# An expert stage whose engines keep a written order, with eight pairs of split weights instead of five

## The chip, the cores and the metric

The kernel runs on one core of one Trainium2 chip. The metric is the device time of one execution in microseconds (us). Inputs and outputs are float32.

## The reference

One encoder layer: a token mixer (attention beside a gated linear recurrence, merged by gates), then a feed-forward part of 16 experts, in which each expert picks its 128 tokens. The change is in the second part alone:

```python
def expert_choice_ffn(h, w_router, w_gate, w_up, w_down):      # S = 1024 tokens, D = 1024, FF = 2048
    cap = EC_CAPACITY_FACTOR * S // N_EXPERTS                   # 128
    affinity = jax.nn.softmax(logits, axis=-1)
    top_w, top_idx = lax.top_k(affinity.transpose(0, 2, 1), cap)
    xe = jax.vmap(lambda hb, ib: hb[ib])(h, top_idx)            # 16 x 128 x 1024
    hid = jax.nn.silu(jnp.einsum('becd,edf->becf', xe, w_gate)) * jnp.einsum('becd,edf->becf', xe, w_up)
    ye = jnp.einsum('becf,efd->becd', hid, w_down) * top_w[..., None]
    # ye is added to the tokens it came from
```

## The kernel before

**Units.** The expert weights come in 768 units of 128 x 1024 float32 (512 KB): for each of 16 experts 16 units of the gate matrix, 16 of up, 16 of down. An expert is worked in two halves of its FF dimension, so a half has 8 units of each kind. For each unit `eunit` (L1153) loads a raw tile (SyncE's queue, L56), and `split` (L89, L90) makes two tiles of it: `eh`, a cast by ScalarE, and `el` = raw - `eh`, by VectorE. TensorE then does 6 matmuls of 128 x 512: high x high, high x low and low x high, for two column halves. For gate and up they are in `wide` (L1255 to L1257, into PSUM tiles `pg`), for down in `down` (L1218 to L1220, into `py`).

**Buffers.** Raw units go round a ring of 26 tiles (7 of tag `er`, 16 of tag `H`, 3 of tag `er3`); 4 more units are loaded ahead into tiles that later serve for something else (`ye`, `xh`, `xl`, `xg`). Of `eh` and `el` there are 5 pairs (`EB`).

**Other steps of an expert.** `pick` (L1195) makes a one-hot matrix `oh` on VectorE, multiplies it on TensorE (L1202) to get the token indices `idx`, and starts an indirect DMA on GpSimd's queue that gathers the 128 tokens into `xg`. `trans(xg, 8, "x")` turns them on TensorE (8 transposes, L1184, into `tp`) and makes `xh` on ScalarE (L1188) and `xl` on VectorE (L1189), in 8 pieces each; here this is called the x turn. After the gate units of a half, ScalarE makes silu (L1273, `hd`); after its up units VectorE multiplies (L1284). `trans(hd, 4, "h")`, twice in a half, turns the result (8 transposes) and makes `hh` (ScalarE, L89) and `hl` (VectorE, L90); this is the h turn. After the second half's down units VectorE scales `py` into `ye` (L1225), and GpSimd's queue adds it to the output by an indirect DMA (L1226).

**Order.** The program is written gate, down of the half before, up (L1266 on); the h turn is called between gate units 4 and 5, the x turn after the up units of an expert's second half. But in this stage a scheduler orders each engine's instructions by its own estimates, so that what stands in a row on an engine can differ from what is written. Each engine then works through its row in that order, and an instruction that waits holds up all that stand behind it.

Of the kernel before, what the change touches and what calls it, by code (L numbers as in the profile page):

```python
# [9 lines left out]
F32 = mybir.dt.float32  # L10
# [27 lines left out]
def trunk(ctx, tc, t, out, dbg=None):  # L38
# [966 lines left out]
    ER, E3, EB, YB = 7, 3, 5, 1  # L1005

    X2 = dict(er3=E3, ye=YB, xh=2, xl=2)
# [137 lines left out]
    NR = ER + 16 + E3  # L1145
# [3 lines left out]
    def eunit(src):  # L1149
        shape = [P] + list(src.shape)[1:]  # L1150
        j = cnt[0] if cnt[0] < NR else cnt[0] - len(ahead)
        c = j % NR
        if NR <= cnt[0] < NR + len(ahead):  # L1153
            raw = ahead[cnt[0] - NR]
        elif c < ER:
            raw = exr.tile(shape, F32, name="er", bufs=ER)
        elif c >= ER + 16:
            raw = exr.tile(shape, F32, name="er3", tag="er3", bufs=E3)
        else:
            raw = h4("er2", shape, F32)  # L1160
        if not NR <= cnt[0] < NR + len(ahead):
            load(raw, src)
        cnt[0] += 1
        hi = ex1.tile(shape, F32R, name="eh", bufs=EB)
        lo = ex1.tile(shape, F32R, name="el", bufs=EB)
        with ExitStack() as es:
            if cnt[0] <= EB:
                es.enter_context(tc.issue_after(first5[-2]))
                es.enter_context(tc.issue_after(first5[-1]))
            if 3 < cnt[0] <= 24:  # L1170
                es.enter_context(tc.issue_after(held[0]))
            if EB < cnt[0] <= 24:
                es.enter_context(tc.issue_after(held[8]))
            split(raw, hi, lo, nc.gpsimd if cnt[0] <= 3 else None)
        return hi, lo

    def trans(src, n, tag):
        pool = exr if tag == "x" else ex
        hi = pool.tile([P, n, P], F32R, name=tag + "h", tag=tag + "h", bufs=2)
        lo = pool.tile([P, n, P], F32R, name=tag + "l", tag=tag + "l", bufs=2)  # L1180
        for g in range(0, n, 4):
# [3 lines left out]
            if tag == "x":  # L1185
                for c in range(4):
                    k = g + c
                    held.append(nc.scalar.activation(hi[:, k], p[:, c], AF.Identity, bias=mcT[:, k:k + 1], scale=1.0).ins)  # L1188
                    nc.vector.scalar_tensor_tensor(lo[:, k], p[:, c], mcT[:, k:k + 1], hi[:, k].bitcast(F32),  # L1189
                                                   op0=ALU.add, op1=ALU.subtract)  # L1190
            else:
                split(p, hi[:, g:g + 4], lo[:, g:g + 4])
        return hi, lo

    def pick(e):  # L1195

        oh = ex.tile([P, NT, P], BF16, name="oh", bufs=1)
        nc.vector.tensor_tensor(oh, slots[:, None, :].to_broadcast([P, NT, P]),
                                slot[:, :, e:e + 1].to_broadcast([P, NT, P]), ALU.is_equal)
        pi = psE.tile([P, 512], F32, name="tp", bufs=2)  # L1200
# [4 lines left out]
        xg = ex.tile([P, D], F32, name="xg", tag="xg", bufs=2)  # L1205
# [3 lines left out]

    def down(e, fp, hTs, py, ks):  # L1210

        for kk in ks:
            hh, hl = hTs[kk // 4]
            r = kk % 4
            wh, wl = eunit(dunit(e, (fp * 8 + kk) * P))
# [5 lines left out]
        if fp == 1 and ks[-1] == 7:  # L1221
            ye = exr.tile([P, D], F32, name="ye", tag="ye", bufs=YB)
            for n in range(2):
                sl = slice(n * 512, (n + 1) * 512)
                nc.vector.scalar_tensor_tensor(ye[:, sl], py[:, n], tw[:, e:e + 1], g2b[:, sl], op0=ALU.mult, op1=ALU.mult)  # L1225
            nc.gpsimd.indirect_dma_start(out=out, out_offset=bass.IndirectOffsetOnAxis(ap=idx[:, e:e + 1], axis=0),  # L1226
                                         in_=ye, in_offset=None, compute_op=ALU.add)
# [8 lines left out]
    for tag, n, src in (("ye", YB, dunit(0, 2 * P)), ("xh", 2, dunit(0, 3 * P)), ("xl", 2, dunit(0, 4 * P)),  # L1236
                        ("xg", 2, dunit(0, 5 * P))):
# [4 lines left out]
    with tc.high_priority(300):  # L1242
        xparts = trans(pick(0), KT, "x")

    def wide(e, w, fp, parts, between=None):

        xh, xl = parts
        ps = [psE.tile([P, 512], F32, name="pg", bufs=4) for _ in range(2)]
        for k in range(KT):
            if between and k == 4:  # L1250
                between()
            wh, wl = eunit(gunit(e, w, fp, k))
            for n in range(2):
                sl = slice(n * 512, (n + 1) * 512)
                nc.tensor.matmul(ps[n], xh[:, k], wh[:, 0, sl], start=k == 0, stop=False)  # L1255
                nc.tensor.matmul(ps[n], xh[:, k], wl[:, 0, sl], start=False, stop=False)  # L1256
                nc.tensor.matmul(ps[n], xl[:, k], wh[:, 0, sl], start=False, stop=k == KT - 1)  # L1257
        return ps

    def turned(hds):  # L1260
        return [trans(hd, 4, "h") for hd in hds]

    pend = None
    py = None
    for e in range(NE):
        mine = xparts  # L1266
        for fp in range(2):
            turn = []
            gs = wide(e, wg_, fp, mine, (lambda: turn.extend(turned(pend[2]))) if pend else None)
            acts = []  # L1270
            for n in range(2):
                hd = ex.tile([P, 512], F32, name="hd", tag="hd", bufs=3)
                nc.scalar.activation(hd, gs[n], AF.Silu)  # L1273
                acts.append(hd)
            last = e == NE - 1 and fp == 1
            if fp == 0 and e + 1 < NE:
                xg = pick(e + 1)
            if pend and not last:
                if pend[1] == 0:
                    py = psE.tile([P, 2, 512], F32, name="py", bufs=1)  # L1280
                down(pend[0], pend[1], turn, py, range(8))
            us = wide(e, wu_, fp, mine)
            for n in range(2):
                nc.vector.tensor_tensor(acts[n], acts[n], us[n], ALU.mult)  # L1284
            if fp == 1 and e + 1 < NE:
                xparts = trans(xg, KT, "x")
            if last:
                py = psE.tile([P, 2, 512], F32, name="py", bufs=1)
                down(pend[0], pend[1], turn, py, range(4))
                t0 = trans(acts[0], 4, "h")  # L1290
                down(pend[0], pend[1], turn, py, range(4, 8))
# [45 lines left out]
```

## Time and profile before

| | us |
|---|---|
| runs: median (lowest to highest) | 2306.76 (2303.48 to 2307.94) |
| the profiled execution, its device time | 2305.64 |
| its span, first to last instruction | 2303.8 |
| expert stage in it: first gate matmul to last down matmul | 1132.36 to 2291.83 |
| TensorE busy in the span | 2150.1 (93%) |
| VectorE busy | 1868.5 (81%) |
| ScalarE busy | 1383.3 (60%) |

The profile names TensorE's matmuls PE, VectorE DVE, ScalarE ACT, GpSimd POOL and SyncE's queue SPq. A time of an instruction is its start from the begin of the span. Matmuls overlap in the pipeline, so what one costs is read from start to start, not from its duration.

### The profile page before, as it was taken

How to read it: one execution, taken by the hardware profiler on the slowest of the kernel's cores; microseconds unless marked ns; L12 is line 12 of the kernel's file. 1: busy time of each engine (PE TensorE's matmuls, PEld its weight loads, DVE VectorE, ACT ScalarE, POOL GpSimd, SP SyncE). 2: the span in 40 equal slices, each digit the busy share in tenths (PEclk: the TensorE clock that was granted, in tenths of full speed). 3: DMA queues.
4: the chain of work that ended last, by engine and by line, in shares of the span. 5: the costliest groups of instructions: out<-in, count | busy, mean ns of one | idle time of the engine just before them, and what ended most of it. 6: DMA issues, size and time to landing. Idle time of an engine off the chain costs nothing.

```text
span 2303.8 us, 30740 instructions
## 1 busy us (share of the span) xinstructions
PE 2150.1 (93%) x10518; PEld 1718.9 (75%) x10518; DVE 1868.5 (81%) x2601; ACT 1383.3 (60%) x2051; POOL 363.9 (16%) x341
## 2 busy tenths in 40 slices
PE   5998888999999999998499999999999999999997
PEld 4775665788888768897377877778777777777776
DVE  7699998588756465728899999999888898888886
ACT  4657666544433122224477777777777776777675
POOL 5247666000000000005200000000100000000000
PEclk9999999999999999999699999999999999999999
DMA  8111111422231885458589999999999999999992
GB/s 290 58 40 38 38 37 33 142 89 78 97 96 65 257 280 177 136 181 284 181 325 385 365 360 362 369 381 372 338 352 360 367 352 364 354 347 369 355 337 85
DMA packets 208246, 546.84 MB, mean 237 GB/s; under 512 B 19589, under 2 KB 75429, under 8 KB 208090
## 3 DMA queue, kind: packets, MB, share of 16 engines
q1 hardware_dynamic: 185242, 495.08, 59.4%
q0 software_dynamic: 8416, 29.41, 4.5%
q10 hardware_dynamic: 14432, 20.39, 2.5%
q8 instruction: 82, 1.34, 0.2%
q14 instruction: 74, 0.61, 0.1%
HBM read 503.80 MB, written 41.01 MB: 236 GB/s over the span
## 4 chain that ended last, share of the span: by engine, by line
PE 68%; DVE 14%; issue 7%; DMA 5%; ACT 4%; POOL 1%; SPq 0%; ACTq 0%; POOLq 0%; DVEq 0%
PE pg L1256 9%; PE pg L1257 9%; PE pg L1255 9%; PE py L1219 5%; PE py L1220 5%; PE py L1218 4%; DVE Tl L90 3%; PE g L208 2%; PE g L210 2%; PE s L711 2%; PE g L209 2%; DMA wr<-in_ada_w 2%; DVE el L90 2%; DVE mx L567 2%; ACT eh L89 1%
## 5 line engine op out<-in xcount | busy, mean ns | idle before, releaser
L90 DVE TENSOR_TENSOR el<-er,eh 128x1024 fp32r<-128x1024 f32 x761 | 898.1, 1220 | 66.3 <-ACT eh L89 54.6
L89 ACT CAST eh<-er 128x1024 fp32r<-128x1024 f32 x764 | 780.2, 1052 | 144.2 <-PE pg L1257 102.4
L1256 PE MATMUL pg<-el,xh 128*128 128x512 f32 x1024 | 412.0, 403 | 8.6 <-DVE el L90 7.5
L1257 PE MATMUL pg<-eh,xl 128*128 128x512 f32 x1024 | 402.1, 397 | 0.3
L1255 PE MATMUL pg<-eh,xh 128*128 128x512 f32 x1024 | 367.6, 399 | 3.6 <-ACT xh L1188 3.4
L1256 PEld LDWEIGHTS pg<-el,xh 128*128 128x128 f32 x1024 | 192.5, 188 | 65.0 <-DVE el L90 21.7
L1255 PEld LDWEIGHTS pg<-eh,xh 128*128 128x128 f32 x1024 | 192.4, 188 | 53.5 <-ACT xh L1188 7.8
L1257 PEld LDWEIGHTS pg<-eh,xl 128*128 128x128 f32 x1024 | 191.3, 188 | 48.2 <-DVE xl L1189 7.4
L1219 PE MATMUL py<-el,hh 128*128 128x512 f32 x512 | 202.8, 396 | 7.6 <-DVE el L90 7.6
L1218 PE MATMUL py<-eh,hh 128*128 128x512 f32 x512 | 201.5, 394 | 0.8 <-ACT eh L89 0.5
L1220 PE MATMUL py<-eh,hl 128*128 128x512 f32 x512 | 199.8, 390 | 0.0
L208 PE MATMUL g<-hTh,wh 128*128 128x512 f32 x448 | 179.8, 401 | 5.0 <-ACT wh L89 2.9
L210 PE MATMUL g<-hTh,wl 128*128 128x512 f32 x448 | 179.6, 401 | 0.3 <-DVE wl L90 0.2
L209 PE MATMUL g<-hTl,wh 128*128 128x512 f32 x448 | 178.8, 399 | 0.0
L1206 POOL DMA_INDIRECT xg<-d_h,idx x16 | 29.1, 1821 | 804.4 <-DVE idx L1203 678.2
L90 DVE TENSOR_TENSOR Tl<-E,Th 128x512 fp32r<-128x512 f32 x128 | 134.2, 1071 | 2.2 <-ACT Th L89 2.1
L638 POOL TENSOR_TENSOR sum<-sum,E 128x512 f32<-128x512 f32 x84 | 128.2, 1526 | 25.4 <-ACT E L632 20.4
L1219 PEld LDWEIGHTS py<-el,hh 128*128 128x128 f32 x512 | 96.0, 188 | 35.7 <-DVE el L90 15.6
L1218 PEld LDWEIGHTS py<-eh,hh 128*128 128x128 f32 x512 | 96.1, 188 | 25.1 <-ACT eh L89 5.1
L228 ACT ACTIVATE stg<-g 128x512 f32<-128x512 f32 (+1 forms) x78 | 45.1, 578 | 109.3 <-PE g L210 70.1
L1220 PEld LDWEIGHTS py<-eh,hl 128*128 128x128 f32 x512 | 96.2, 188 | 18.8
L90 DVE TENSOR_TENSOR wl<-wr,wh 128x1024 fp32r<-128x1024 f32 x56 | 68.6, 1227 | 43.9 <-ACT wh L89 43.9
(336 smaller groups left out, 3912.3 us busy)
## 6 DMA issues: line engine op xcount, KB each, us to landing
er<-in_w_exp_gate SPq DMA_DIRECT2D x256, 512.0 KB
er<-in_w_exp_up SPq DMA_DIRECT2D x256, 512.0 KB
er<-in_w_exp_down SPq DMA_DIRECT2D x252, 512.0 KB
wr<-in_w_in SPq DMA_DIRECT2D x42, 512.0 KB
wr<-in_ada_w SPq DMA_DIRECT2D x32, 512.0 KB
d_sg<-stg ACTq DMA_DIRECT2D x32, 256.0 KB
sg<-d_sg SPq DMA_DIRECT2D x16, 512.0 KB
d_zq<-stg ACTq DMA_DIRECT2D x24, 256.0 KB
```

The lines of the kernel that those rows point to most:

```text
L89: first = nc.scalar.copy(hi, src)
L90: (eng or nc.vector).tensor_tensor(lo, src, hi.bitcast(F32), ALU.subtract)
L208: nc.tensor.matmul(p, wh[:, k], xT(hTh, n, k), start=k == 0, stop=False)
L209: nc.tensor.matmul(p, wh[:, k], xT(hTl, n, k), start=False, stop=False)
L210: nc.tensor.matmul(p, wl[:, k], xT(hTh, n, k), start=False, stop=k == KT - 1)
L638: (nc.vector if j == NH - 1 else nc.gpsimd).tensor_tensor(a, acc, E, ALU.add)
L1218: nc.tensor.matmul(py[:, n], hh[:, r], wh[:, 0, sl], start=fp == 0 and kk == 0, stop=False)
L1219: nc.tensor.matmul(py[:, n], hh[:, r], wl[:, 0, sl], start=False, stop=False)
L1220: nc.tensor.matmul(py[:, n], hl[:, r], wh[:, 0, sl], start=False, stop=fp == 1 and kk == 7)
L1255: nc.tensor.matmul(ps[n], xh[:, k], wh[:, 0, sl], start=k == 0, stop=False)
L1256: nc.tensor.matmul(ps[n], xh[:, k], wl[:, 0, sl], start=False, stop=False)
L1257: nc.tensor.matmul(ps[n], xl[:, k], wh[:, 0, sl], start=False, stop=k == KT - 1)
```

## The change

It does four things, all in the expert stage.

- **Written order.** The stage becomes a `script`: a list of units and of acts between them. It is emitted inside `in_order(PE, DVE, Activation)`, which ties each instruction of these three engines to the one before it in program order. The split of unit j is emitted in front of unit m as soon as the unit that had its pair before is one of those in front of m (`ensure`).
- **Gate, up, down.** A half is now 8 gate units, silu, 8 up units, the multiply, then the 8 down units of the half before. The h turn stands between up units 4 and 5. The x turn stands between down units 4 and 5 of the half before the one that uses it, and `pick` at the same place one half earlier. `oh` is made after the gate units.
- **Eight pairs.** Five pairs of `eh`, `el` stay as they are; three more take the 7 tiles of tag `er` after the first 7 raw units have left them. The raw ring is then 19 tiles (16 `H`, 3 `er3`); the first 26 loads go where they went. `xg` has one buffer instead of two, so 3 units are loaded ahead instead of 4; `hd` has four instead of three.
- **The x turn's pieces.** All 8 transposes come first, then 8 pieces of `xh`, then 8 of `xl`, instead of `xh` and `xl` by turns.

The number of matmuls, splits, unit loads and indirect DMAs stays the same.

```diff
-    ER, E3, EB, YB = 7, 3, 5, 1
+    EB, MORE, YB = 5, 3, 1
+    RAW = dict(er=7, er3=3)
+    TAGS = ["er"] * 7 + ["H"] * 16 + ["er3"] * 3
+    RING, PAIR = ["H"] * 16 + ["er3"] * 3, "er"
+    PAIRS0 = 7
...
+    def eload(src):
+        shape = [P] + list(src.shape)[1:]
+        j = cnt[0]
+        cnt[0] += 1
+        if NR <= j < NR + len(ahead):
+            return ahead[j - NR]
+        tag = TAGS[j] if j < NR else RING[(j - NR - len(ahead)) % len(RING)]
+        raw = h4("er2", shape, F32) if tag == "H" else exr.tile(shape, F32, name=tag, bufs=RAW[tag])
+        load(raw, src)
+        return raw
+
+    def pair_tag(j):
+        return PAIR if j >= PAIRS0 and (j - PAIRS0) % (EB + MORE) >= EB else None
...
+    def eparts(raw, j):
+        tag = pair_tag(j)
+        if tag:
+            hi, lo = (exr.tile(shape, F32R, name=n, tag=tag, bufs=RAW[tag]) for n in ("eh", "el"))
         else:
+            hi, lo = (ex1.tile(shape, F32R, name=n, bufs=EB) for n in ("eh", "el"))
...
+            split(raw, hi, lo, nc.gpsimd if j < 3 else None)
...
+    for h in range(NH2):
+        e, fp = divmod(h, 2)
+        more = e + 1 < NE
+        for k in range(KT):
+            wide_unit(e, wg_, h, (h, 0), k)
+        act(lambda h=h: silu(h))
+        if more and not fp:
+            act(lambda e=e: set_(ohs, e + 1, lambda: onehot(e + 1)))
+        for k in range(KT):
+            if k == 4:
+                if h:
+                    act(lambda h=h: (turn(h - 1, 0), turn(h - 1, 1)))
+                else:
+                    act(lambda: set_(xgs, 1, lambda: pick(1, ohs[1])))
+            wide_unit(e, wu_, h, (h, 1), k)
+        act(lambda h=h: gated(h))
+        for kk in range(8) if h else ():
+            if kk == 4 and more:
+                if fp:
+                    act(lambda e=e: set_(xparts, e + 1, lambda: trans(xgs[e + 1], KT, "x")))
+                else:
+                    act(lambda e=e: set_(xgs, e + 1, lambda: pick(e + 1, ohs[e + 1])))
+            if kk in (4, 6) and h == NH2 - 1:
+                act(lambda n=kk // 2 - 2: turn(h, n))
+            down_unit(h - 1, kk)
+    for kk in range(8):
+        down_unit(NH2 - 1, kk)
...
+    def ensure(done):
+        while len(parts_) < len(srcs) and before[len(parts_)] < done:
+            parts_.append(eparts(eload(srcs[len(parts_)]), len(parts_)))
...
+    ensure(0)
+    with in_order(ET.PE, ET.DVE, ET.Activation):
+        j = 0
+        for z, run in script:
+            if z is None:
+                run()
+            else:
+                ensure(j)
+                run(*parts_[j])
+                j += 1
```

What this does to the engines' rows is shown at two places. The first is ScalarE's row around the h turn of a late half. A number behind a name tells tiles apart; `er`, `er2` and `er3` are raw tiles. Before:

```order
L89 CAST eh_17673<-er2_17671 128x1024
L89 CAST eh_17685<-er3_17683 128x1024
L89 CAST eh_17697<-er3_17695 128x1024
L89 CAST hh_17719<-tp_17721 128x512
L89 CAST hh_17728<-tp_17730 128x512
L89 CAST eh_17709<-er3_17707 128x1024
L89 CAST eh_17739<-er_17737 128x1024
```

TensorE turns `tp_17721` in the middle of the unit of `eh_17685`, the second gate unit: that unit and one more are split ahead of the turn's cast, and the fourth gate unit's split, `eh_17709`, stands behind it.

After, the same turn of the same engine:

```order
L89 CAST eh_17817<-er2_17815 128x1024
L89 CAST eh_17831<-er2_17829 128x1024
L89 CAST eh_17843<-er2_17841 128x1024
L89 CAST eh_17855<-er2_17853 128x1024
L89 CAST hh_17865<-tp_17867 128x512
L89 CAST hh_17874<-tp_17876 128x512
L89 CAST eh_17885<-er3_17883 128x1024
```

TensorE now turns `tp_17867` behind the fourth up unit, that of `eh_17763`. The seven units that follow on TensorE are split ahead of the turn's cast: four up units (the last is that of `eh_17817`) and three down units (`eh_17831`, `eh_17843`, `eh_17855`).

The second place is TensorE's row around the x turn. Before (expert 6, and so in experts 1 to 6):

```order
L1256 MATMUL pg_14142<-el_14230,xh_13561 128x512
L1257 MATMUL pg_14142<-eh_14229,xl_13562 128x512
L1184 MATMUL tp_14243<-ident_69,xg_13722 128x128 x4
L1184 MATMUL tp_14256<-ident_69,xg_13722 128x128 x4
L1255 MATMUL pg_14269<-eh_14273,xh_14241 128x512
L1256 MATMUL pg_14269<-el_14274,xh_14241 128x512
```

After, an expert's x turn and the matmuls around it:

```order
L1281 MATMUL py_16912<-eh_16858,hl_16839 128x512
L1202 MATMUL tp_16957<-ident_69,xg_16632 128x128 x4
L1202 MATMUL tp_16962<-ident_69,xg_16632 128x128 x4
L1279 MATMUL py_16912<-eh_16870,hh_16847 128x512
L1280 MATMUL py_16912<-el_16871,hh_16847 128x512
...
L1281 MATMUL py_16912<-eh_16908,hl_16848 128x512
L1265 MATMUL pg_17037<-eh_16921,xh_16955 128x512
```

The turn stood right in front of the gate matmul that reads `xh`; now four down units stand between them.

## Rows read from the trace of the kernel before

**Rows 1.** Busy time by stretch of the expert stage (us; in brackets the number of instructions; then the granted TensorE clock as a share of full speed, the mean busy share of the 16 DMA engines, and GB/s). Columns: stretch, its length, PE, PEld, DVE, ACT, POOL.

```profile
1132.36:1200.00 67.64, 67.05 (x301) 53.27 (x300) 60.78 (x69) 54.47 (x67) 1.75 (x1) 0.98 0.82 295
1200.00:1600.00 400.00, 397.06 (x1802) 317.55 (x1801) 373.51 (x386) 316.41 (x358) 24.15 (x12) 1.00 0.99 369
1600.00:2200.00 600.00, 585.52 (x2620) 459.47 (x2619) 530.19 (x568) 442.62 (x530) 34.66 (x16) 1.00 0.97 356
```

**Rows 2.** The same view for one expert each, cut where two successive x turns begin on TensorE: one of the earlier experts, one of the later.

```profile
1404.11:1475.35 71.24, 70.65 (x321) 56.40 (x320) 66.52 (x70) 56.36 (x64) 4.11 (x2) 1.00 0.99 369
1880.98:1954.34 73.36, 71.68 (x322) 56.17 (x320) 64.93 (x70) 53.95 (x65) 4.04 (x2) 1.00 0.99 359
```

**Rows 3.** Waits of SyncE's queue in 1150 to 2304 us (what waited, for whom: us in total, times, longest).

```profile
SPq L56 <- DVE el L90: 704.4, 628, 6.5
```

**Rows 4.** TensorE without a wait: the view by stretch (TensorE alone; us busy, instructions that touch the stretch, clock, DMA share, GB/s) for 72 gate and up matmuls and for 48 down matmuls, each with one that began before; then the instructions in order of time (start, length, what) around an h turn and around a pick.

```profile
1429.95:1446.75 16.80, 16.80 (x73) 1.00 1.03 377
1453.24:1464.14 10.90, 10.90 (x49) 1.00 1.03 410
...
1446.76 1.03 PE L1184 MATMUL tp<-ident,hd 128*128 128x128 f32 x8
1447.55 0.48 PE L1255 MATMUL pg<-eh,xh 128*128 128x512 f32 x1
1447.87 0.40 PE L1256 MATMUL pg<-el,xh 128*128 128x512 f32 x1
...
1418.75 0.35 PE L1202 MATMUL tp<-tq,oh 128*128 128x5 bf16 x8
1418.96 0.47 PE L1218 MATMUL py<-eh,hh 128*128 128x512 f32 x1
1419.28 0.39 PE L1219 MATMUL py<-el,hh 128*128 128x512 f32 x1
```

**Rows 5.** Instructions in order of time as in Rows 4: TensorE from the x turn of an earlier expert to its next h turn; 24 gate matmuls lie between.

```profile
1404.11 1.04 PE L1184 MATMUL tp<-ident,xg 128*128 128x128 f32 x8
1405.68 0.50 PE L1255 MATMUL pg<-eh,xh 128*128 128x512 f32 x1 [0.53 <-ACT xh L1188]
...
1412.27 1.04 PE L1184 MATMUL tp<-ident,hd 128*128 128x128 f32 x8
```

**Rows 6.** Instructions in order of time for a later expert; in brackets the idle time before, and what ended it. First ScalarE and TensorE around an h turn, then VectorE and TensorE around the end of an expert's down units.

```profile
1909.49 1.05 ACT L89 CAST eh<-er 128x1024 fp32r<-128x1024 f32 x1 [0.35 <-PE pg L1257]
1914.60 1.08 ACT L89 CAST hh<-tp 128x512 fp32r<-128x512 f32 x2 [4.05 <-PE tp L1184]
...
1913.96 1.04 PE L1184 MATMUL tp<-ident,hd 128*128 128x128 f32 x8
...
1923.97 0.40 PE L1218 MATMUL py<-eh,hh 128*128 128x512 f32 x1
1924.40 0.50 PE L1256 MATMUL pg<-el,xh 128*128 128x512 f32 x1
1924.74 0.39 PE L1257 MATMUL pg<-eh,xl 128*128 128x512 f32 x1
...
1936.77 1.41 DVE L1225 SCALAR_TENSOR_TENSOR ye<-py,tw,g2b 128x512 f32<-128x512 f32 x2 [1.51 <-PE py L1220]
...
1939.36 0.50 PE L1256 MATMUL pg<-el,xh 128*128 128x512 f32 x1 [0.77 <-DVE el L90]
```

**Rows 7.** The costliest groups of instructions from 1350 us on (shapes, count; us busy, mean ns of one; idle before, and what ended it).

```profile
L90 DVE TENSOR_TENSOR el<-er,eh 128x1024 fp32r<-128x1024 f32 x620 | 728.6, 1220 | 52.0 <-ACT eh L89 45.3
L89 ACT CAST eh<-er 128x1024 fp32r<-128x1024 f32 x619 | 628.4, 1052 | 103.9 <-PE pg L1257 75.4 <-PE py L1220 25.2 <-ACT xh L1188 1.7
L90 DVE TENSOR_TENSOR hl<-tp,hh 128x512 fp32r<-128x512 f32 x52 | 34.9, 684 | 0.4 <-ACT hh L89 0.3
L1284 DVE TENSOR_TENSOR hd<-hd,pg 128x512 f32<-128x512 f32 x52 | 33.4, 683 | 34.3 <-PE pg L1257 34.3
L1189 DVE SCALAR_TENSOR_TENSOR xl<-tp,mcT,xh 128x128 fp32r<-128x128 f32 x96 | 31.7, 344 | 0.0
L1225 DVE SCALAR_TENSOR_TENSOR ye<-py,tw,g2b 128x512 f32<-128x512 f32 x28 | 19.7, 746 | 16.4 <-PE py L1220 16.4
L1198 DVE TENSOR_TENSOR oh<-slots,slot 128x1024 bf16<-128x1024 bf16 x10 | 12.1, 1214 | 0.0
```

**Rows 8.** The view by stretch again (columns as in Rows 1), 71 us cut by how the DMA engines are used.

```profile
1357.00:1363.00 6.00, 6.00 (x28) 4.87 (x27) 5.73 (x7) 4.47 (x5) 1.53 (x1) 1.00 1.03 414
1363.00:1372.00 9.00, 9.00 (x40) 7.25 (x39) 8.69 (x10) 6.80 (x7) 0.79 (x1) 1.00 1.03 341
1372.00:1402.00 30.00, 30.00 (x135) 24.48 (x134) 27.15 (x24) 23.85 (x26) 0.00 (x0) 1.00 1.03 410
1402.00:1428.00 26.00, 25.41 (x122) 19.60 (x121) 24.71 (x32) 20.99 (x29) 1.79 (x1) 1.00 0.92 317
```

**Rows 9.** The stage's begin and end in order of time; the issues of the down units' loads (count; shortest, median and longest ns; first and last start in us) and the casts after the last of them (stretch, length, busy, count, clock, DMA share, GB/s); and the page's line on the gathers (KB or median us from issue to landing).

```profile
1132.36 0.79 PE L1255 MATMUL pg<-eh,xh 128*128 128x512 f32 x1
...
1134.94 0.39 PE L1255 MATMUL pg<-eh,xh 128*128 128x512 f32 x1
...
2291.83 0.39 PE L1220 MATMUL py<-eh,hl 128*128 128x512 f32 x1
...
L56 SPq DMA_DIRECT2D er<-in_w_exp_down x248: 327/328/441, 1156.0 to 2252.7; - x124
...
2260.00:2290.00 30.00, 20.19 (x21) 1.00 0.00 1
...
xg<-d_h,idx POOLq DMA_INDIRECT x16, 8.8
```

More of the change, by code (lines that the diff above doesn't have):

```diff
@@ L1184, in trans, with onehot @@
                 nc.tensor.transpose(p[:, c], src[:, (g + c) * P:(g + c + 1) * P], ident)
[L1185 to L1192, printed above, removed]
+            ps.append(p)
+        if tag == "x":
+            for k in range(n):
+                held.append(nc.scalar.activation(hi[:, k], ps[k // 4][:, k % 4], AF.Identity, bias=mcT[:, k:k + 1],
+                                                 scale=1.0).ins)
+            for k in range(n):
+                nc.vector.scalar_tensor_tensor(lo[:, k], ps[k // 4][:, k % 4], mcT[:, k:k + 1], hi[:, k].bitcast(F32),
+                                               op0=ALU.add, op1=ALU.subtract)
+        else:
+            split(ps[0], hi, lo)
         return hi, lo
-    def pick(e):
+    def onehot(e):
         oh = ex.tile([P, NT, P], BF16, name="oh", bufs=1)
@@ L1208, in pick, with gunit, dunit, unit @@
         return xg
[L1210 to L1215, printed above, removed]
+    def gunit(e, w, fp, k):
+        return w[e, k * P:(k + 1) * P, fp * 1024:(fp + 1) * 1024].rearrange("(k p) n -> p k n", p=P)
+    def dunit(e, r0):
+        return wd_[e, r0:r0 + P].rearrange("(k p) n -> p k n", p=P)
+    for tag, n, src in (("ye", YB, gunit(0, wu_, 1, 2)), ("xh", 2, gunit(0, wu_, 1, 3)), ("xl", 2, gunit(0, wu_, 1, 4))):
+        a = (exr if tag in X2 else ex).tile([P] + list(src.shape)[1:], F32, name="ahead", tag=tag, bufs=n)
+        load(a, src)
+        ahead.append(a)
+    script = []
+    def unit(src, run):
+        script.append((src, run))
+    def act(run):
+        script.append((None, run))
+    xparts, hds, hTs, pys, xgs, ohs, banks = {}, {}, {}, {}, {}, {}, {}
+    def wide_unit(e, w, h, key, k):
+        def run(wh, wl):
+            if k == 0:
+                banks[key] = [psE.tile([P, 512], F32, name="pg", bufs=4) for _ in range(2)]
+            xh, xl = xparts[e]
+            for n in range(2):
+                sl = slice(n * 512, (n + 1) * 512)
+                p = banks[key][n]
+                nc.tensor.matmul(p, xh[:, k], wh[:, 0, sl], start=k == 0, stop=False)
+                nc.tensor.matmul(p, xh[:, k], wl[:, 0, sl], start=False, stop=False)
+                nc.tensor.matmul(p, xl[:, k], wh[:, 0, sl], start=False, stop=k == KT - 1)
+        unit(gunit(e, w, h % 2, k), run)
+    def down_unit(h, kk):
+        e, fp = divmod(h, 2)
+        def run(wh, wl):
+            if fp == 0 and kk == 0:
+                pys[e] = psE.tile([P, 2, 512], F32, name="py", bufs=1)
+            py, (hh, hl), r = pys[e], hTs[h, kk // 4], kk % 4
             for n in range(2):
@@ L1242, in trunk @@
-    with tc.high_priority(300):
[L1243 to L1291, printed above, removed]
-                down(e, 1, [t0, trans(acts[1], 4, "h")], py, range(8))
-            pend = (e, fp, acts)
@@ new lines, in run @@
+            if fp == 1 and kk == 7:
+                ye = exr.tile([P, D], F32, name="ye", tag="ye", bufs=YB)
+                for n in range(2):
+                    sl = slice(n * 512, (n + 1) * 512)
+                    nc.vector.scalar_tensor_tensor(ye[:, sl], py[:, n], tw[:, e:e + 1], g2b[:, sl], op0=ALU.mult, op1=ALU.mult)
+                nc.gpsimd.indirect_dma_start(out=out, out_offset=bass.IndirectOffsetOnAxis(ap=idx[:, e:e + 1], axis=0),
+                                             in_=ye, in_offset=None, compute_op=ALU.add)
@@ new lines, in down_unit, with silu, gated, turn @@
+        unit(dunit(e, (fp * 8 + kk) * P), run)
+    def silu(h):
+        hds[h] = []
+        for n in range(2):
+            hd = ex.tile([P, 512], F32, name="hd", tag="hd", bufs=4)
+            nc.scalar.activation(hd, banks[h, 0][n], AF.Silu)
+            hds[h].append(hd)
+    def gated(h):
+        for n in range(2):
+            nc.vector.tensor_tensor(hds[h][n], hds[h][n], banks[h, 1][n], ALU.mult)
+    def turn(h, n):
+        hTs[h, n] = trans(hds[h][n], 4, "h")
+    def set_(d, k, f):
+        d[k] = f()
```

63 lines of the change are left out of this document (23 added, 40 removed).

## The prediction

> **What bounds the kernel now.** The page's busy shares come first, since they say where to look: TensorE 93% of the span. The view by stretch shows where the rest goes. In the expert stage TensorE works 397.1 of 400 us up to 1600, but 585.5 of 600 from there on [rows 1]. Cut by expert, an earlier one takes 71.24 us and a later one 73.36 [rows 2]. In front of 1131 us the rows of TensorE, VectorE, ScalarE and GpSimd are the same before and after, so the whole question is what the 1159.7 us from the first gate matmul (1132.36) to the end of the last down matmul (2291.83 + 0.23) can shrink to.
>
> What would an expert take if TensorE never waited? Read it where it doesn't wait [rows 4]. 72 gate and up matmuls take 16.80 us, 0.2333 each; 48 down matmuls 10.90, or 0.2271. Eight transposes and the matmul behind them take 1447.87 - 1446.76 = 1.11 us, so a turn costs 1.11 - 0.23 = 0.88. A pick costs 0.53 - 0.23 = 0.30. An expert has 192 x 0.2333 = 44.80, 96 x 0.2271 = 21.80, three turns = 2.64 and a pick: **69.5 us**. So an earlier expert loses 1.7 us and a later one 3.8.
>
> Where an earlier one loses it: between the x turn at 1404.11 and the h turn at 1412.27 lie 8.16 us for work of 0.88 + 24 x 0.2333 = 6.48 [rows 5]. That is 1.68, the whole loss: the first gate matmuls wait for `xh` and `xl`, which come in pieces by turns from two engines.
>
> Where a later one loses it: ScalarE finishes a cast at 1910.54 and then stands idle 4.05 us, because the next instruction in its row is the h turn's cast, and TensorE makes that turn only at 1913.96 [rows 6]. The pairs that TensorE frees meanwhile stay unsplit. Ten us later TensorE pays: it makes one down matmul at 1923.97, goes back to gate matmuls at 1924.40, and waits on `el`. The second place is the end of an expert's down units: VectorE stands 1.51 us at `ye`, and TensorE waits for the `el` behind it, 0.77 us by the profile (1939.36) [rows 6].
>
> Loads are not late. SyncE's queue waits 704 us for raw tiles to be split [rows 3]; the last load is issued at 2252.7, and 21 casts are still to come after 2260, when the DMA engines are idle [rows 9]. Some 20 units lie landed and unsplit at that point.
>
> **The change, part by part.** *Eight pairs.* A pair is free when its unit ends on TensorE. The cast starts 0.35 us later [rows 6], takes 1.05, and `el` 1.22 [rows 7]: 2.6 us. With five pairs the next unit of that pair is due four units on, 4 x 1.40 = 5.6 us, so ScalarE or VectorE may be held up 3.0 us before TensorE waits. 4.05 exceeds this. With eight pairs it is seven units, 9.8 us, and 7.2 us may be lost.
>
> *Written order.* The turn's cast now stands behind the casts of seven units that TensorE needs first, and the unit whose pair frees next comes right behind it. ScalarE reaches it about when TensorE makes the turn: the row of before shows the cast 0.64 us behind the first transpose (1914.60 - 1913.96) [rows 6], so that is all it can wait. `ye` and the multiply may still hold VectorE some 1.5 us, inside the 7.2. I sum up the worst pile on VectorE near the x turn: multiply 1.37, eight `xl` 2.75, a wait of about 1.0 for the first `xh` (my estimate, from 0.64 and a piece of `xh`), less what it makes good on four units, 4 x (1.40 - 1.22) = 0.7: 4.4 us, under 7.2. So 3.8 us of a later expert go.
>
> *The x turn four units ahead.* TensorE does not need `xh` until 4 x 6 x 0.2271 = 5.4 us after the turn, and a piece every 1.40 us from there. Eight `xl` of 0.344 are done in 2.75 us plus the 4.4 - 2.75 above. The cover is those four units and VectorE's lag; without it the 1.68 of [rows 5] comes back. So 1.7 us of an earlier expert go.
>
> *What is moved past queues.* `pick` and its gather on GpSimd's queue go half an expert ahead of the turn that reads them: 24 units, 34 us, for a landing of 8.8 [rows 9]. One `xg` is enough, since the turn that read it last lies as far back. The scatter of `ye` comes behind the gather on that queue and nothing waits for it. SyncE's queue keeps its 768 loads in the order of use. Cost nothing, all three.
>
> *Fewer raw tiles.* 19 instead of 26, and one unit less loaded ahead. Of the 20 units that lie ready some 13 remain, 18 us of work. Cost nothing while the loads keep pace.
>
> *Do the others keep pace?* VectorE is busy 66.5 us per expert [rows 2], of 69.5. Near, but it holds. DMA: an expert is 369 GB/s x 71.24 us = 26.3 MB. In the 45 us where the engines are full they move 414, 341 and 410 GB/s, 397 in the mean with a scatter inside [rows 8]: 26.3 MB in 66.2 us, and about 2 more for a gather (my estimate, from the 341 stretch). 68 of 69.5. In the rest of [rows 8] they have less to do (317 GB/s), because splits are late. Nothing is bound below 69.5, but VectorE and the DMA engines come within 3 us of it.
>
> A rule speaks against this. The Trainium skill (DMA: Bandwidth & Descriptors, "Where 436 GB/s comes from") says that transfers from HBM are held at about 358 GB/s a core, and the 356 of the late experts looks like it [rows 1]. But 410 GB/s over 30 us [rows 8] disagrees, so I take it as a rival and not as the bound.
>
> **The sum.** Sixteen experts of 44.80 + 21.80 + 1.76 + 0.30 = 68.66 make 1098.6; 15 x turns at 0.88 add 13.2, one pick less takes 0.3; the first unit, at half clock, takes 2.58 instead of 1.40 [rows 9], 1.2 more. 1112.7 us against 1159.7: 47.0 gone if nothing is left. I leave 0.1 us per expert for the small waits that I can't name, 1.6. The profiled execution's 2305.64 becomes 2260.2, and the median of the runs lies 1.1 above that execution: **2261 us**. What follows the last matmul (`ye`, its scatter) stays.
>
> **Rivals.**
>
> *A DMA ceiling* (0.10). If the DMA engines can't exceed the 361 GB/s that they average from 1200 to 2200 [rows 1], the last load is issued at 2252.7 as before. Now no stock is left: the load's landing, some 3 us, a split, 2.3, and its unit, 1.4, end TensorE at 2259.4, not 2292.1: 32.7 gone, 2274. For it: share 0.97 to 0.99 all along. Against: [rows 8]. By the skill's figure it would be about the same.
>
> *Waits of the earlier kind stay* (0.14). VectorE has 71.24 - 66.52 = 4.7 us idle in an earlier expert. If it keeps half or all of this, because its written row still stops at `hh`, `xh` and `py`, an expert takes 69.5 + 0.9 to 71.24: 14 to 28 us more than forecast, 2275 to 2288.
>
> *The change doesn't reach TensorE* (0.03): the three further pairs come free late, as their tiles are shared, and the new order puts other waits in place of the old: within 0.2% of now.
>
> *Slower* (0.04): VectorE becomes the bound. Added up without overlap its instructions are 48 x 1.220 + 4 x 0.684 + 4 x 0.683 + 8 x 0.344 + 2 x 0.746 + 1.21 = 69.5 us an expert [rows 7]. With a strict row that keeps the 4.7 us of waits that is 74.2, and 16 x (74.2 - 69.5) = 75 over the forecast: 2336. It is slower than now from 72.5 us per expert on. Against it: the row's instructions overlap, 66.5 us busy for the same work [rows 2], and a late VectorE finds what it waits for done.
>
> **How the numbers follow.** Forecast 0.69, between 2256 and 2268: the lower end is no wait at all less a matmul step 0.2% shorter, the upper end 0.5 us per expert. The range reaches to the DMA ceiling and into the third case, to 2283, and to 2255 below; about 0.16 is left out. What a measurement can tell from no change is about 0.2%, 4.6 us: faster 0.93, same 0.03, slower 0.04.
>
> **What would show it.** Right: an expert period of 69.5 to 70 us between x turns from the first to the last; TensorE busy over 99% from 1140 to the end; ScalarE's idle time before `hh` under 1 us; no gap behind the x turn; a DMA rate near 378 GB/s. DMA ceiling: a rate that stays near 361, and loads that wait less for raw tiles. VectorE the bound: its busy share over 97% and waits of TensorE for `el` in every half. Wrong at the root: periods of 71 us and more with the same waits at the new places.

## The result

| | before | after |
|---|---|---|
| median of 4 runs each on one chip (lowest to highest), us | 2307.35 (2303.48 to 2308.11) | 2255.66 (2251.34 to 2258.15) |
| profiled execution, us | 2305.64 | 2256.22 |
| its span, us | 2303.8 | 2254.4 |

The ratio is 0.9777, 95% interval [0.9758, 0.9796]: 2.2% faster. The forecast was 2261, the range 2255 to 2283.

The view by stretch of the changed kernel (columns as in [rows 1]: stretch, length, PE, PEld, DVE, ACT, POOL, clock, DMA share, GB/s), first the two long stretches, then one expert each from x turn to x turn:

```profile
1200.00:1600.00 400.00, 400.00 (x1848) 326.40 (x1847) 377.12 (x396) 314.00 (x366) 24.62 (x12) 1.00 1.00 380
1600.00:2200.00 600.00, 600.00 (x2765) 489.83 (x2764) 565.64 (x599) 473.26 (x556) 34.33 (x17) 1.00 1.00 378
1393.00:1462.36 69.36, 69.36 (x321) 56.62 (x320) 65.41 (x71) 54.69 (x64) 4.11 (x2) 1.00 1.00 379
1878.58:1947.95 69.37, 69.37 (x322) 56.62 (x320) 65.42 (x71) 54.70 (x64) 4.11 (x2) 1.00 1.00 380
```

Where [rows 1] had 397.06 of 400 us and 585.52 of 600, TensorE is now busy all the time, and where [rows 2] had 71.24 and 73.36, early and late experts both take 69.37. The stage's first gate matmul and its last down matmul:

```profile
1131.34 0.79 PE L1265 MATMUL pg<-eh,xh 128*128 128x512 f32 x1
...
2242.26 0.40 PE L1281 MATMUL py<-eh,hl 128*128 128x512 f32 x1
```

So the stage takes 2242.26 + 0.23 - 1131.34 = 1111.2 us instead of 1159.7: 48.5 of the span's 49.4 us. It also starts 1.0 earlier, and what follows it is 0.2 longer.

The view of waits from 1132 us on (what waited, for whom: us in total, times, longest) names no matmul, and of the weight loads, beside those of the picks (0.4 us at most), one: 0.7 us at the start. It and what the other engines wait:

```profile
ACT eh L89 <- PE pg L1267: 94.4, 202, 1.6
DVE el L90 <- ACT eh L89: 44.8, 130, 1.6
ACT hd L1295 <- PE pg L1267: 28.3, 31, 0.9
ACT hh L89 <- PE tp L1202: 25.1, 32, 0.8
...
ACT hh L89 <- PE py L1280: 3.3, 1, 3.3
...
PEld pg L1267 <- DVE xl L1209: 0.7, 1, 0.7
...
SPq L56 <- DVE el L90: 740.7, 715, 4.1
```

ScalarE's wait at `hh` was 4.05 us in [rows 6]; now none of 32 is over 0.8, and one of 3.3 is in the last half, where no gate units follow. The last row, from SyncE's queue (1150 to 2250 us), is the counterpart of [rows 3]: loads still wait for raw tiles to be split, though there are fewer tiles.

The same turns in order of time: ScalarE, VectorE and TensorE around an x turn, then ScalarE around an h turn.

```profile
1393.63 2.18 ACT L1206 ACTIVATE xh<-tp,mcT 128x128 fp32r<-128x128 f32 x8 [0.75 <-PE tp L1202]
...
1394.82 2.16 DVE L1209 SCALAR_TENSOR_TENSOR xl<-tp,mcT,xh 128x128 fp32r<-128x128 f32 x8 [0.64 <-ACT xh L1206]
...
1393.79 0.47 PE L1279 MATMUL py<-eh,hh 128*128 128x512 f32 x1
1399.38 0.39 PE L1265 MATMUL pg<-eh,xh 128*128 128x512 f32 x1
...
1416.72 1.08 ACT L89 CAST hh<-tp 128x512 fp32r<-128x512 f32 x2 [0.79 <-PE tp L1202]
```

TensorE goes from the turn straight to down matmuls. All `xl` pieces are done at 1396.98, the gate units begin at 1399.38: the four units' cover has 2.4 us to spare.

### The profile page after: what moved, and what is told of

It reads as the page before. It is cut to its first block, busy times and chain, and to the rows that moved or that the text cites. A ratio compares the mean times of both kernels' runs of the same rounds, so it can differ in the third digit from the quotient of the medians.

```text
span 2254.4 us, 30907 instructions
## 1 busy us (share of the span) xinstructions
PE 2123.6 (94%) x10518; PEld 1726.7 (77%) x10518; DVE 1862.4 (83%) x2601; ACT 1378.7 (61%) x2051; POOL 364.5 (16%) x341
## 4 chain that ended last, share of the span: by engine, by line
PE 74%; DVE 11%; DMA 5%; issue 5%; ACT 2%; POOL 1%; SPq 0%; POOLq 0%; ACTq 0%; DVEq 0%
PE pg L1267 10%; PE pg L1266 10%; PE pg L1265 10%; PE py L1279 5%; PE py L1281 5%; PE py L1280 5%; DVE Tl L90 3%; PE g L208 2%; PE g L210 2%; PE s L711 2%; PE g L209 2%; DMA wr<-in_ada_w 2%; PE tp L1202 2%; DVE mx L567 2%; PE s L929 1%
## 5 line engine op out<-in xcount | busy, mean ns | idle before, releaser
L90 DVE TENSOR_TENSOR el<-er,eh 128x1024 fp32r<-128x1024 f32 x762 | 888.4, 1219 | 49.1 <-ACT eh L89 44.8
L1265 PE MATMUL pg<-eh,xh 128*128 128x512 f32 x1024 | 405.8, 396 | 0.0
L1266 PE MATMUL pg<-el,xh 128*128 128x512 f32 x1024 | 403.2, 394 | 0.0
```

What stands on the lines that cost most here:

```text
L90: (eng or nc.vector).tensor_tensor(lo, src, hi.bitcast(F32), ALU.subtract)
L1265: nc.tensor.matmul(p, xh[:, k], wh[:, 0, sl], start=k == 0, stop=False)
L1266: nc.tensor.matmul(p, xh[:, k], wl[:, 0, sl], start=False, stop=False)
```

## The experiments

Twelve kernels ran, each four to ten times but for one. Each group shared a chip with runs of the kernel before, whose medians there were 2303 to 2304; the ratios are to these.

**Is it the pairs or the order?** Four runs with the changed kernel as their base. *five_pairs* takes the three further pairs away and gives their tiles back to the raw ring; *four_pairs* takes away one more (`4, 0, 1` in the same line):

```diff
-    EB, MORE, YB = 5, 3, 1
+    EB, MORE, YB = 5, 0, 1
-    RING, PAIR = ["H"] * 16 + ["er3"] * 3, "er"
+    RING, PAIR = TAGS, "er"
```

*own_order* keeps eight pairs and the new program, and lets the scheduler order the rows; *own_order_five* is both edits.

```diff
-    with in_order(ET.PE, ET.DVE, ET.Activation):
+    with ExitStack():
```

> The changed kernel with 5 pairs instead of 8 and all 26 raw tiles in the ring; order of units and acts as changed. Theory (hold-ups against the lead of the pairs): a hold-up of up to 3.0 us is free with five pairs; only the pile at the x turn, 2.5 to 4.4 us, goes beyond it, so 0 to 1.5 us an expert come back, expert period 69.4 to 70.9 us, 2256 to 2280 us in all, and any wait of TensorE sits behind the x turn. Rival (the pairs bring it): the later experts' 73.4 us come back, 2300 us or more.

> The changed kernel without the tie between instructions: eight pairs, the new program order and 19 raw tiles, but the scheduler orders each engine. Theory (order is what matters): waits for the turns' casts come back where the scheduler puts them early, and the x turn moves next to the gate matmuls; some of 1.7 to 3.8 us an expert returns, 2265 to 2300 us. Rival (depth is what matters): with a lead of 7.2 us a hold-up of 4.05 us is free, the period stays at 69.4 to 69.6 us, 2256 to 2260 us.

> The changed kernel's program with five pairs and a raw ring of 26 tiles, and no tie between neighbours in program order: the scheduler orders each engine's row again. It completes the square of order by pairs. Theory, the order brings the gain and pairs only soften hold-ups of a scheduled row: eight pairs in scheduled order gave 2297, so with five the waits grow, 2298 to 2312 us, periods of 73 to 74 us late in the stage. Rival, pairs have no part in either order: 2294 to 2299 like the run with eight. Second rival, the scheduler finds a better row when it has fewer pairs to plan ahead with: under 2290.

> Written order, four pairs in all, raw ring of 26. A pair that comes free is due again three units later, 4.2 us, less 2.6 for the cast and el: a hold-up of 1.6 us may be lost. Theory (the lead has to cover the hold-ups that the written order leaves, and these are 1 to 2 us at the x turn, the h turn and ye): waits of 1 to 4 us per expert appear at these places, periods of 70.5 to 73.5, the kernel 2274 to 2322 us. Rival, the written order leaves no hold-up that TensorE feels: 69.65 us an expert as with five pairs, 2258 to 2264. Second rival, with so short a lead every unit is late: over 2340.

| us, median; ratio to before | scheduler's order | written order |
|---|---|---|
| eight pairs | 2297.27; 0.9973 [0.9961, 0.9984] | 2255.66; 0.9777 [0.9758, 0.9796] |
| five pairs | 2293.31; 0.9958 [0.9942, 0.9974] | 2260.21; 0.9807 [0.979, 0.9823] |
| four pairs | not run | 2261.18; 0.9819 [0.9802, 0.9836] |

The order brings nearly all of it; the pairs bring nothing by their number. With five pairs no matmul waits either; an expert takes 69.65 us instead of 69.37, and this is in the matmuls: the view by stretch for 72 gate and up matmuls, TensorE alone, of the changed kernel and of five_pairs:

```profile
1399.38:1416.08 16.70, 16.70 (x73) 1.00 0.97 363
```

```profile
1404.05:1420.85 16.80, 16.80 (x74) 1.00 0.95 352
```

Four pairs, whose lead by the prediction's arithmetic is 1.6 us, give 69.71, as the rival of *four_pairs* said; its theory of 1 to 4 us of waits fell. VectorE at an x turn of four_pairs, and the weight load that waits for it behind:

```profile
1394.60 2.16 DVE L1209 SCALAR_TENSOR_TENSOR xl<-tp,mcT,xh 128x128 fp32r<-128x128 f32 x8 [0.45 <-ACT xh L1206]
...
1397.94 0.19 PEld L1280 LDWEIGHTS py<-el,hh 128*128 128x128 f32 x1 [0.20 <-DVE el L90]
```

A hold-up is still there: VectorE is away from the splits for 0.45 + 2.16 = 2.6 us. That is more than 1.6, and yet one weight load an expert is 0.20 late, which puts off one matmul by 0.05 (1398.29 - 1398.01 = 0.28 instead of 0.23). So the arithmetic gives too short a lead; by how much no run shows.

In the scheduler's order eight pairs don't help. Early experts of own_order run without a wait, at 69.36; late ones are back at 73.1:

```profile
1324.84:1394.20 69.36, 69.36 (x321) 56.62 (x320) 64.39 (x70) 52.70 (x62) 4.44 (x2) 1.00 1.00 379
1797.59:1870.71 73.12, 71.91 (x321) 55.44 (x320) 65.08 (x70) 52.16 (x64) 4.10 (x2) 1.00 0.98 359
```

Its waits from 1132 us on, and ScalarE in order of time around one late h turn:

```profile
ACT hh L89 <- PE py L1280: 137.6, 34, 5.6
ACT hd L1295 <- PE pg L1267: 68.2, 30, 6.6
PE pg L1266 <- DVE el L90: 11.2, 31, 0.6
```

```profile
1831.33 0.59 ACT L89 CAST hh<-tp 128x512 fp32r<-128x512 f32 x1 [5.56 <-PE py L1280]
1831.82 3.89 ACT L89 CAST eh<-er 128x1024 fp32r<-128x1024 f32 x4
1837.47 0.59 ACT L89 CAST hh<-tp 128x512 fp32r<-128x512 f32 x1 [1.77 <-PE py L1280]
```

The row stands at `hh` for 5.56 us and, six later, for 1.77 again, where [rows 6] had 4.05. It stands for something else, too: in [rows 6] the cast waited for the turn, here the turn is long made. TensorE around it:

```profile
1826.55 0.60 PE L1202 MATMUL tp<-ident,hd 128*128 128x128 f32 x4
...
1830.90 0.39 PE L1280 MATMUL py<-el,hh 128*128 128x512 f32 x1
```

There are two `hh` tiles, and the cast waits until four down units have read one of them. No run gives the scheduler more `hh` tiles, so how much of its loss hangs on these two is open.

The same program with five pairs, own_order_five, waits less there:

```profile
ACT hh L89 <- PE py L1280: 97.3, 33, 3.8
```

So with more pairs the scheduled row stands longer at this cast. In time the difference is small (2293 against 2297, and the intervals overlap). Of the expectations for own_order_five the first rival, that pairs have no part in either order (2294 to 2299), comes nearest; against its theory the waits at `hh` didn't grow, and 2293 is above what the second rival said (under 2290).

What these runs leave open is which part of the written order is needed: none ties ScalarE's row alone, and none ties the program as it was written before.

**The order of the three kinds.** *down_second* writes each half as gate, down of the half before, up. The h turn then stands in the gate units, the x turn and `pick` between up units 4 and 5, and the three units loaded ahead follow the new order; all else is as changed.

```diff
         act(lambda h=h: silu(h))
...
+        for kk in range(8) if h and not last else ():
+            down_unit(h - 1, kk)
...
-        for kk in range(8) if h else ():
+        for kk in range(8) if last else ():
```

> The changed kernel with the units in the order of before: gate, down of the half before, up; h turn in the gate units, x turn and pick between up units 4 and 5; all tied, eight pairs. Theory: the order of the three kinds alone is worth nothing, since no operand is needed sooner than four units behind the step that makes it, and the lead is the same: period 69.3 to 69.6 us, within 4 us of the changed kernel. Rival (gate, up, down is what spreads the work of ScalarE and VectorE): waits at silu and the multiply come back, 0.5 us or more an expert, 8 us or more in all.

2254.1 us, ratio 0.9789 [0.9771, 0.9807], 69.4 us an expert. Gate, up, down is worth nothing by itself.

**The x turn.** *x_late* puts it directly in front of the gate units; *x_late_turns* has in addition the pieces `xh`, `xl` by turns, as before the change.

```diff
         for kk in range(8) if h else ():
             if kk == 4 and more:
-                if fp:
-                    act(lambda e=e: set_(xparts, e + 1, lambda: trans(xgs[e + 1], KT, "x")))
-                else:
+                if not fp:
                     act(lambda e=e: set_(xgs, e + 1, lambda: pick(e + 1, ohs[e + 1])))
...
+        if more and fp:
+            act(lambda e=e: set_(xparts, e + 1, lambda: trans(xgs[e + 1], KT, "x")))
```

> The changed kernel with the x turn right in front of the next expert's gate units, behind all eight down units. Theory: TensorE waits there for xh and xl as before; the pieces of each kind now come without a pause, so it is less than the 1.68 us of before: 0.7 to 1.2 us for the first piece of xh and xl on each of 15 turns, and the later pieces are in time; period 70.1 to 70.6 us, 11 to 18 us longer in all, 2267 to 2274 us. Rival (the turn's cost before was the pieces by turns, not the place): no wait longer than 0.3 us, within 5 us of the changed kernel.

> The x turn directly in front of the gate units that read it, as in the run of that kind, and its pieces xh, xl by turns as before the change. Theory (the 1.68 us that an earlier expert of the kernel before lost behind its x turn is the late place and the pieces by turns together): the gap behind the turn is 1.5 to 1.8 us instead of 0.78, an expert takes 70.9 to 71.3 us, the kernel 2277 to 2287 us. Rival, the order of the pieces is nothing and the kernel before lost the rest to something else: 70.2 to 70.6 us, 2266 to 2273, as with the late turn alone.

x_late: 2268.81 us, 0.985 [0.9834, 0.9867], 70.37 an expert, as its theory said. x_late_turns: 2259.47, 0.9809 [0.979, 0.9828], 69.65: it missed both of its expectations, on the low side. By turns is the better way at the late place. TensorE behind the turn, in order of time, in x_late and then in x_late_turns:

```profile
1399.45 0.50 PE L1265 MATMUL pg<-eh,xh 128*128 128x512 f32 x1
1399.79 0.40 PE L1266 MATMUL pg<-el,xh 128*128 128x512 f32 x1
1400.61 0.50 PE L1267 MATMUL pg<-eh,xl 128*128 128x512 f32 x1 [0.43 <-DVE xl L1209]
```

```profile
1399.69 0.50 PE L1264 MATMUL pg<-eh,xh 128*128 128x512 f32 x1
1400.03 0.39 PE L1265 MATMUL pg<-el,xh 128*128 128x512 f32 x1
1400.26 0.39 PE L1266 MATMUL pg<-eh,xl 128*128 128x512 f32 x1
```

The third matmul comes 0.82 us behind the second in one, 0.23 in the other. So pieces by turns can't have cost the kernel before its 1.68 us [rows 5]. What did is in its own trace: VectorE around that turn in order of time, and what TensorE's weight loads wait for there (1404 to 1413):

```profile
1404.93 1.22 DVE L90 TENSOR_TENSOR el<-er,eh 128x1024 fp32r<-128x1024 f32 x1
1406.07 0.60 DVE L1189 SCALAR_TENSOR_TENSOR xl<-tp,mcT,xh 128x128 fp32r<-128x128 f32 x2
1406.59 1.22 DVE L90 TENSOR_TENSOR el<-er,eh 128x1024 fp32r<-128x1024 f32 x1
1407.72 0.60 DVE L1189 SCALAR_TENSOR_TENSOR xl<-tp,mcT,xh 128x128 fp32r<-128x128 f32 x2
...
1409.65 0.60 DVE L1189 SCALAR_TENSOR_TENSOR xl<-tp,mcT,xh 128x128 fp32r<-128x128 f32 x2
```

```profile
PEld pg L1257 <- DVE xl L1189: 1.2, 3, 0.5
PEld pg L1255 <- ACT xh L1188: 1.2, 2, 0.8
```

The scheduler put a whole split of 1.22 us behind every two pieces, and in the compiled row the pieces stand as 0, 4, 1, 5, 2, 6, 3, 7: of each two, TensorE needs only one next. So it got one needed piece each 1.65 to 1.93 us and wanted one each 1.40. The 24 matmuls behind the turn took 6.59 us instead of 5.60, and they began 0.69 late. No run takes the splits and the order of the pieces apart.

**What would bound it next.** *two_products* leaves out the third product of each unit (low activations by high weights), so that TensorE has 4 matmuls a unit.

```diff
-                nc.tensor.matmul(p, xh[:, k], wl[:, 0, sl], start=False, stop=False)
-                nc.tensor.matmul(p, xl[:, k], wh[:, 0, sl], start=False, stop=k == KT - 1)
+                nc.tensor.matmul(p, xh[:, k], wl[:, 0, sl], start=False, stop=k == KT - 1)
```

(and the same for down.)

> Leaves out the third product of each unit (low activations by high weights), so TensorE has 4 matmuls a unit instead of 6, some 47 us an expert, and no longer sets the pace; splits, loads and order stay. It shows what would bound the kernel next. Prediction's terms: VectorE 66.5 us and the DMA engines 66 to 68 us an expert. If the DMA engines decide at the rate seen before over 45 us (397 GB/s): 66 to 68 us an expert and 397 GB/s. If VectorE decides: 66 to 67, its busy share over 98%, DMA share under 1. If transfers are held near 358 GB/s: 73 us and more an expert, which the changed kernel's 378 GB/s already speaks against.

One run, 2181.42 us. The view by stretch:

```profile
1239.64:1303.63 63.99, 55.43 (x225) 37.33 (x224) 63.99 (x70) 53.09 (x64) 20.01 (x2) 0.97 1.03 402
2018.17:2085.35 67.18, 56.71 (x226) 37.06 (x225) 64.86 (x71) 55.57 (x65) 15.46 (x2) 0.97 1.02 399
```

TensorE has waits in both. First VectorE decides, at 64.0 us an expert without a pause, less than the 66 to 67 expected; later it pauses too, an expert takes 64.9 to 67.6, and ScalarE waits for loads (the longest of three such rows, from 1600 to 2100 us):

```profile
ACT eh L89 <- DMA er<-in_w_exp_up: 25.2, 70, 1.4
```

**Why a matmul steps 0.2333 us.** A step is the time from one matmul's start to the next. five_pairs raised the question, since in the changed kernel gate and up matmuls with a raw-tile pair were faster. Such a matmul has a stationary operand (128 x 128 of `xh` or `xl`, loaded by PEld) and a moving one (128 x 512 of `eh` or `el`). The start addresses in SBUF (from the compiled programs) against the starts of matmuls in the trace gave the first guess, near or far. *x_left* has three fixed pairs instead of five and moves `xh`, `xl` to the pool `ex` beside them; *x_left5* moves them too, with five fixed pairs, none in raw tiles (`5, 0, 1`), and a raw ring of 22.

```diff
-    EB, MORE, YB = 5, 3, 1
+    EB, MORE, YB = 3, 3, 1
...
-        pool = exr if tag == "x" else ex
+        pool = ex
```

> Fixed pairs three instead of five, and the parts xh, xl of the tokens lie where the other two pairs lay, so that stationary and moving operand of a gate or up matmul come from other places in SBUF than in the changed kernel; six pairs in all, the same order, the same work. In the changed kernel's trace a gate or up matmul that reads xh, xl against a fixed pair steps by 0.2333 us, against a pair in the raw tiles by 0.227 to 0.229, and a down matmul by 0.2267. Theory A, the step hangs on where the two operands lie: with xh, xl moved beside the fixed pairs the gate and up matmuls step by 0.227 to 0.229 too; an expert takes 68.4 to 69.0 us instead of 69.4, the kernel 2240 to 2251 us. Theory B, the step hangs on what the matmul is (gate and up against down), and the short step of pairs in the raw tiles is something else of those tiles: the gate and up step stays near 0.2333 for fixed pairs and the period at 69.3 to 69.6, the kernel 2254 to 2260. Rival on depth: six pairs allow a hold-up of 4.4 us, and five pairs were enough, so no waits from that.

> Five fixed pairs and none in the raw tiles, and xh, xl beside these pairs instead of beside the raw tiles (raw ring of 22 tiles in place of 19, three units of the prefetch less at the start). Theory A (the step of 0.2333 comes from xh, xl and a fixed pair lying far from each other in SBUF): all gate and up matmuls step by about 0.227, an expert takes about 68.3 to 68.6 us, the kernel 2240 to 2246. Theory B (the step belongs to gate and up whatever the place): 0.2333 for all, 69.65 us an expert as with five pairs, 2258 to 2264. A smaller prefetch can cost up to 2 us at the start of the stage under either.

x_left: 2248.3, 0.9766 [0.9748, 0.9784], 69.0 an expert. x_left5: 2239.71, 0.9728 [0.9711, 0.9744], 68.31. Theory B, that the step belongs to gate and up, fell. Theory A had both times, x_left5 to within 0.3 us, but in x_left 72 matmuls took 16.54 us, 0.2297 each and not 0.2267, though `xh` and `xl` lay beside three of the six pairs. So *shift64* moved one pool by 64 bytes, and *before_shift192*, in the kernel before, by 192 (48 floats).

```diff
+    gap = ctx.enter_context(tc.tile_pool(name="gap", bufs=1, side="right"))
+    gap_t = gap.tile([P, 16], F32, name="gap")
+    nc.gpsimd.memset(gap_t, 0.0)
     exr = ctx.enter_context(tc.tile_pool(name="exr", bufs=1, side="right"))
```

> The changed kernel with one 64-byte tile in front of the pool of the raw tiles, xh and xl: all tiles of that pool lie 64 bytes lower, and every operand of the experts' matmuls then starts at the same remainder of 128 bytes (64); in the changed kernel xh, xl and the three pairs in raw tiles start at remainder 0, and the five fixed pairs, hh and hl at 64. Nothing else differs: same order, same eight pairs, same loads. Theory A, the matmul's step hangs on where in SBUF the operands lie (near or far): no change, 69.3 to 69.5 us an expert, 2253 to 2259. Theory C, it hangs on the two operands' starts against each other modulo 128 bytes: all matmuls step by 0.2267, an expert takes 68.3 us, the kernel 2237 to 2243 us. Against C speaks the run with three fixed pairs and xh, xl beside them, whose operands at the same remainder did not step by 0.2267 throughout.

> The kernel before the change, with a tile of 192 bytes in front of the pool of the raw tiles, xh and xl, and nothing else: xh, xl and the pairs of eh, el then start at the same remainder of 128 bytes (64), but at different remainders of 256 and 512 (448 and 64 of 512). It asks two things. Which remainder: if equal starts modulo 128 are enough, 72 gate and up matmuls without a wait take 16.3 us (0.2267 each) instead of 16.80; if it has to be 256 or more, they stay at 16.7 to 16.8 and the kernel at 2300 to 2310 us. And what a shorter step is worth in a kernel whose TensorE waits: if waits and step add up, each expert gains 192 x 0.0067 = 1.28 us, an earlier one takes 69.96 and a later one 72.1, the kernel 2282 to 2287 us; if the held-up rows of ScalarE and VectorE set the pace of the later experts, these stay at 73.0 to 73.4, only the earlier ones gain, and the kernel takes 2291 to 2299 us.

shift64: **2238.04** (2236.36 to 2241.03), 0.972 [0.9704, 0.9737], 68.31 an expert: the fastest, 17.6 us under the changed kernel's median, by one tile of 64 bytes (the medians are of two chips; sixteen experts of 1.06 us less make 17.0). before_shift192: 2302.68, 0.9995 [0.9985, 1.0004]. 72 gate and up matmuls in shift64, then in before_shift192 (columns as for five_pairs):

```profile
1393.17:1409.50 16.33, 16.33 (x73) 1.00 1.01 374
```

```profile
1426.46:1443.20 16.74, 16.74 (x74) 1.00 1.02 365
```

Near or far is refuted, as nothing moved but 64 bytes. Equal starts modulo 128, my theory C, are not enough either: 16.74 is barely under 16.80 [rows 4]. What fits all of these is that the starts have to be equal modulo 256 or 512. 72 matmuls without a wait, read as above:

| kernel | starts of `xh`, `xl` and of the pairs, modulo 512 | 72 matmuls, us |
|---|---|---|
| five_pairs | 128; 64 | 16.80 |
| changed | 128; five at 64, three at 128 | 16.70 |
| before_shift192 | 448; 64 | 16.74 |
| x_left | 64; three at 64, three at 128 | 16.54 |
| x_left5 | 64; 64 | 16.32 |
| shift64 | 64; 64 | 16.33 |

The in-between time of x_left has its reason in the steps: behind a unit whose operands start unequally, one that starts alike doesn't step evenly at once. Here that takes two units; in the changed kernel, where the raw-tile pairs start like `xh`, one or two (1380 and 1360 ns, or 1382, 1381 and 1360). The six steps of successive gate units in x_left, `xh` and `xl` at 64 throughout, worked out from matmul starts (ns, and their sum):

```
gate unit, pair at 128: 232 226 229 231 226 229   1373
gate unit, pair at  64: 235 230 234 236 224 231   1390
gate unit, pair at  64: 235 229 232 231 227 226   1380
gate unit, pair at  64: 227 227 226 227 227 226   1360
```

Why unequal starts cost this no run shows, nor which of 256 and 512 it is. What a shorter step is worth in the kernel that waits stays open as well, since before_shift192 hardly shortened it.

## Why the prediction was right, and where its reasons were not

**The dense expert** was right: 69.5 us forecast, 69.37 measured. The missing 0.13 is the step: some units of the three raw-tile pairs fall under 0.2333. In the changed kernel's stage the forecast was 1112.7 + 1.6 = 1114.3 us, and 1111.2 came: the 1.6 left for small waits wasn't needed, and the step gave up to 16 x 0.13 = 2.1. With the start 1.0 earlier that is the 4.0 us between 2260.2 and 2256.22, to within 0.7.

**Written order**: right, and it is the cause. Its absence costs 41.6 us with eight pairs and 33.1 with five.

**Eight pairs** was the step that failed. The prediction explained the late experts by a lead of 3.0 us against a wait of 4.05 and counted on 7.2. The runs show that in the written order four pairs are enough, with a lead of 1.6 by that arithmetic and VectorE held up for 2.6. In the scheduler's order 7.2 is not enough: late experts take 73.1 us. The row waits 5.56 there, which alone is under 7.2, and again 1.77; what else adds to it no run takes apart. The forecast came right without this step, since in the written order fewer pairs do as well.

The pile of 4.4 us on VectorE near the x turn, which I summed up, isn't there. In the changed kernel the wait for `xh` is 0.64 us and the eight `xl` take 2.16, 2.8 in all, and the multiply lies four splits ahead of them:

```profile
1388.36 1.27 DVE L1300 TENSOR_TENSOR hd<-hd,pg 128x512 f32<-128x512 f32 x2
1389.55 4.62 DVE L90 TENSOR_TENSOR el<-er,eh 128x1024 fp32r<-128x1024 f32 x4
```

**The x turn four units ahead**: the amount was right (1.68 gone), the reason was not, so the amount is in part luck. Not pieces by turns cost it, but, as its trace reads, whole splits between them and a row that made later pieces ahead of the next one; the written order takes that away and leaves 69.65 - 69.37 = 0.28 with the turn late. That the pieces now come eight and eight is a loss of 0.72 at the late place (70.37 against 69.65), and the four units ahead cover it.

**Queues, gate-up-down and fewer raw tiles** at nothing: right. With 26 tiles in the ring (five_pairs) no matmul waits, and none with 19.

**VectorE and the DMA engines** were put at 66.5 and 68 us an expert. VectorE does it in 64.0, and 26.3 MB at the 400 GB/s of two_products are 65.8 (my estimate, from one run). The distance to TensorE's 69.4 is thus 5.4 and 3.6 us; the forecast had 3.0 and 1.5.

**The DMA ceiling** didn't come. The DMA engines move 380 and 378 GB/s over 1000 us, and 402 and 399 in two_products. The Trainium skill (DMA: Bandwidth & Descriptors, "Where 436 GB/s comes from") has transfers from HBM bound at about 358 on a core, half of what an HBM stack gives two cores. Here one core is at work, and these stretches are above it. The 356 of [rows 1] was what late splits left to load. **Slower** didn't come either, nor did **waits of the earlier kind**: the rows of ScalarE and VectorE keep waits, but no matmul of an expert waits for them.

## What to carry to other kernels

When an engine in a middle position (here ScalarE) stands idle in front of an instruction that another engine hasn't reached, look first at what stands behind it in its row: moving it behind the work that is needed sooner did here what three more buffers didn't. A wait explained by a count of buffers is tested by taking buffers away, which is cheap; the count fell here at the first run. And when an engine is busy all the time, compare the step of the same instruction in places where nothing waits: two steps for one shape are time that a layout may give back.

## What was not expected of the hardware

At a granted clock of 1.00 the step of a 128 x 512 matmul is 0.2267 us when its stationary and moving operand start at the same remainder of 512 bytes in a partition (16.33 us for 72) and no unequal unit came just before. It is 0.2333 with the stationary one at 128 and the moving one at 64 (16.80), 0.2325 with 448 and 64 (16.74), and 0.2288 with 64 and 128 (1373 ns for six, in x_left). A tile of 64 bytes was worth 1.06 us an expert (69.37 to 68.31), about a third of what the whole change brought.
